# A hybrid attention and S5 layer on one core: S5 tables read from DRAM, work moved around the last gate block, the last unit's normalisations dealt out anew

## The chip, the cores and the metric

The kernel runs on one core of one Trainium2 chip. The metric is the time of one execution on the device in microseconds (us), lower is better. Its engines are TensorE (PE in the profile, with its weight loads as PEld), VectorE (DVE), ScalarE (ACT), GpSimd (POOL) and SyncE (SP), whose DMA queue the profile calls SPq.

## The reference, cut to what matters

```python
for l in range(DEPTH):
    h = _rms_norm(x, pre_norm_g[l])
    z = h @ w_in[l]
    z_q, z_kv, z_kr, g_attn, u_ssm, g_ssm = jnp.split(z, split_points, axis=-1)
    attn = _mla_attention(z_q, z_kv, z_kr, positions, q_norm_g[l], w_uq[l], kv_norm_g[l], w_ukv[l])
    attn = _rms_norm(attn, attn_out_g[l]) * jax.nn.silu(g_attn)
    ssm = _s5_bidirectional(u_ssm, s5_lam_re[l], s5_lam_im[l], s5_log_dt[l], s5_b_re[l], ...)
    ssm = jax.nn.gelu(ssm)
    ssm = ssm * jax.nn.sigmoid(ssm @ w_glu[l] + b_glu[l])
    ssm = _rms_norm(ssm, ssm_out_g[l]) * jax.nn.silu(g_ssm)
    mixed = jnp.concatenate([attn, ssm], axis=-1) @ w_out[l]
    x = x + _rms_norm(mixed, post_norm_g[l])
```

There is one layer, 2048 positions, 1024 channels, all in float32. The attention is MLA: four heads, low-rank queries (256) and keys with values (128), and a rotary key of 64 that all heads share; the softmax runs over all positions. The S5 branch has 32 groups of 16 channels, each with a complex diagonal state of 64, scanned forward and backward.

## The kernel before, in words

Each engine's instructions stand in an order written out by hand: nothing is rescheduled, and each engine takes its own list from top to bottom. A wait therefore holds whatever stands behind it on the same engine. SP issues most of the DMAs, and an issue that waits holds the issues behind it.

**Projections, 0 to 381 us.** `blocks` (line 576) yields, for each pair of tiles of 128 positions, two z blocks, two u blocks (inputs of S5, written to DRAM as `u_d`), and four gate blocks ga0, ga1, gs0, gs1 (`do_gate`, line 332). A gate block is 48 matmuls of TensorE, then a tanh (`tt`) and two scaled copies (`gst`) on ACT, then one DVE operation (line 339), then two stores `g_d<-gst` by SP (line 341). `mm3` (line 208) makes one fp32 product of three matmuls over high and low parts, so most tiles come as a pair such as `zh`, `zl`. Between the blocks, `step` (line 570) advances a generator `tables` that computes the tables of S5 on DVE. Each step adds `BUDGET` (line 50) to what the generator may spend, an amount counted in elements. It stores each table to DRAM (`tab_d`). One step of it needs matmuls, `pc` (line 540), which read scaled tables (`sc`) that DVE writes.

**The seam, 366 to 400 us.** Four quarters of the keys (`keys`, line 675, each in four stages: loads from DRAM, rope, a transposition `ptk` and its split, a transposition `ptr` and its split), the absorbed query weights (`absorbed`, line 588: `pw`, then `wab` and `wqr`) and the first queries (`qprep`, line 712) are threaded between the last gate blocks by a list of `run` calls (lines 800 to 841). The queries' pieces are: a transposition `ptq` of the loaded `zq`, its high part `zh` on ACT and its low part `zl` on DVE; two products `psr` (rope part) and four `psq` (nope part); `ta`, `tb` on DVE; two transpositions `ptr` of `qd` (line 767); and copies to `qo` on ACT and DVE. After `ph1.close()` the memory of the projections is given to the tiles of S5 and attention, so loads into it wait for what used it.

**Attention with S5, 400 to 1120 us.** Each of 256 steps `t` makes one score tile `sc` (five matmuls, lines 1111 to 1115) into one of two PSUM buffers, its maxima on DVE (`nm`, line 1116) and the Exp on ACT (line 1122), so a score tile waits for the Exp two tiles back. Eleven steps later come a transposition (line 1159) and the product with the values (lines 1179 to 1181). `s5_pre` (line 1061) adds S5's work at fixed steps. At its first call it issues the load of the tables (`s5_load`, line 864, one DMA `tab<-tab_d`), the load of the inputs (`u_load`, line 877, eight DMAs `u<-u_d`) and `u_split`, whose copy `uh<-u` on ACT (line 890) waits for all eight. The tables `v` of groups 0 to 3 are made by `v_build` (line 917) on DVE, at steps 0, 1, 3 and 4 (`V_AT`), two products and a sum each; `k_build` (line 931) multiplies them with `Bm` (`pk`, line 938) at step 6 into the lag kernels, which go to DRAM and come back as `m`, split by `m_split` (line 894) into `mh` and `ml`, which the product `py` of S5 reads.

**The end.** After the last score tile, `TAIL` (line 1542) says which engine normalises the last unit's eight tiles `e` (V is DVE, A is ACT, G is POOL), step by step; each is transposed after that (`pt`, line 1159). Then the mixer (gelu, gates, output product) runs to the end.

Of the kernel before, what the change touches and what calls it, by code (L numbers as in the profile page):

```python
# [46 lines left out]
LN2_2 = float(np.float32(math.log(2.0) - LN2_1))  # L47
GELU_C = math.sqrt(2.0 / math.pi)
GELU_A = 0.044715
BUDGET = 1800  # L50
MANUAL = {mybir.EngineType.PE, mybir.EngineType.Activation, mybir.EngineType.DVE, mybir.EngineType.Pool, mybir.EngineType.SP}


# [95 lines left out]
def tile_hymba(ctx, tc, x, pos, inv_freq, pre_g, w_in, q_g, w_uqT, w_uqr, kv_g, w_ukT, w_uv, attn_g,  # L149
# [210 lines left out]
    def s5_params():  # L360
# [63 lines left out]
        while n < T:  # L424
# [12 lines left out]
            n *= 2  # L437
            yield
        sg = Scratch(s5t, [P, NG, GH], "sc")
        for nm, w in (("qr", wr), ("qi", wi)):  # L440
            q = Scratch(s5t, [P, NG, T], "sc")()
            G.tensor_copy(q[0:64], w[0:64, :, 0:T])
            G.tensor_copy(q[64:P], w[64:P, :, 0:T][:, :, ::-1])
            store(nm, q)
        yield

        phi, ph2, ph32 = new("phi"), new("ph2"), new("ph32")
# [140 lines left out]
    def absorbed():  # L588
# [19 lines left out]
            split(wqr_h[:, k, :], wqr_l[:, k, :], raw[:, k, :], qgs[:, k:k + 1])  # L608
        yield


    xt = xp.tile([P, DM], F32, tag="xt", name="xt0")
    halves = [slice(0, 512), slice(512, DM)]
# [22 lines left out]
    for s in range(0, NT, 2):  # L636
        last = s + 2 == NT
        blk = blocks(s)
        for n in range(4 if last else 8):
            next(blk)  # L640
            if s == 0 and n == 0:
                load_w(*BLK[1])
                small_consts()
            if not last and n == 0:
                xs = [load_x(s + 2), load_x(s + 3)]
            if s == 0 and n in (1, 2):
                load_w(*BLK[1 + n])
# [23 lines left out]
    kT_h = kp.tile([P, SEQ], F32R, tag="kT_h", name="kT_h")  # L671
    kT_l = kp.tile([P, SEQ], F32R, tag="kT_l", name="kT_l")
    krS = kp.tile([P, SEQ], F32R, tag="krS", name="krS")

    def keys(q):
        t4 = slice(4 * q, 4 * q + 4)
        c = slice(q * 512, q * 512 + 512)
        zk = stg.tile([P, 4, P], F32, tag="st", name="zk")
        zr = stg.tile([P, 4, 2, HALF], F32, tag="st", name="zr")
        SP.dma_start(zk, z_d[t4, :, 256:384].rearrange("s c d -> c s d"))  # L680
        SP.dma_start(zr.rearrange("p s a b -> p s (a b)"), z_d[t4, :, 384:448].rearrange("s c d -> c s d"))
        yield
        kr2 = stg.tile([P, 4, 2, ROPE], F32, tag="st", name="kr2")
        kab = stg.tile([P, 2, 4, 2, HALF], F32, tag="tt", name="kab", bufs=2)
        V.tensor_tensor(kab[:, 0], zr, bc(ropec[:, t4, :].unsqueeze(2), [P, 4, 2, HALF]), ALU.mult)
        G.tensor_tensor(kab[:, 1], zr[:, :, ::-1, :], ropes[:, t4], ALU.mult)
        d2 = [P, 4, 2, ROPE]
        G.tensor_tensor(kr2, bc(kab[:, 0].rearrange("p s a b -> p s (a b)").unsqueeze(2), d2),
                        bc(kab[:, 1].rearrange("p s a b -> p s (a b)").unsqueeze(2), d2), ALU.add)
        A.activation(kn_h[:, t4, :], zk, AF.Copy)  # L690
        yield
        pt = psT.tile([P, 512], F32, tag="pt", name="ptk")
        for i in range(4):
            PE.transpose(pt[:, i * P:(i + 1) * P], zk[:, i, :], ident)
        split(kT_h[:, c], kT_l[:, c], pt)
        V.tensor_tensor(kn_l[:, t4, :], zk, f32(kn_h[:, t4, :]), ALU.subtract)
        yield
        pr = psZ.tile([P, 512], F32, tag="z", name="ptr")
        for i in range(4):
            PE.transpose(pr[:, i * P:(i + 1) * P], kr2[:, i].rearrange("p a b -> p (a b)"), ident)  # L700
        A.activation(krS[:, c], pr, AF.Copy)
        V.tensor_tensor(krS[64:P, c], pr[64:P, :], f32(krS[64:P, c]), ALU.subtract)
        yield


    zqs = {}
# [82 lines left out]
                    live.remove(i)  # L789
        return out  # L790

    def run(g, n):
        for _ in range(n):
            next(g)


    SP.dma_start(wuv, w_uv)
    ab = absorbed()
    ks = [keys(q) for q in range(4)]
    run(ab, 1)  # L800
    run(ks[0], 1)
    next(blk)
    run(ks[0], 1)
    run(ks[1], 1)
    next(blk)
    run(ab, 1)
    run(ks[0], 2)
    run(ks[1], 1)
    run(ks[2], 1)
    ph1g.close()  # L810
    qp = pool(ph2s, "qp", 6)
    qt_p = pool(ph2q, "qt", 1)
# [4 lines left out]
    run(ab, 1)  # L817
    q0 = qprep(0, psZ, "z")
    next(q0)
    run(ks[2], 1)  # L820
    next(blk)
    run(ks[1], 2)
    run(ks[3], 1)
    V.tensor_scalar(wuv, wuv, kvg, None, ALU.mult)
    run(ab, 1)
    run(q0, 1)
    run(ks[2], 1)
    run(ks[3], 1)
    run(q0, 1)
    next(blk)  # L830
    run(ks[2], 1)
    run(q0, 1)
    run(q0, 1)
    run(ks[3], 1)
    run(q0, 1)
    run(q0, 1)
    run(ks[3], 1)
    run(q0, 1)
    run(q0, 1)
    qo0 = []  # L840
# [76 lines left out]
    def v_build(q, i):  # L917
        f = S5[q]
        vt = s2.tile([P, 2, P], F32, tag="v", name="v", bufs=6)
        tmp = s2.tile([P, 2, P], F32, tag="tmp", name="tmp", bufs=2)  # L920
        two(G if q else V, vt, tmp, f["qr"][:, i, :], f["qi"][:, i, :], f["ct"][:, i, 0:2, :], f["ct"][:, i, 1:3, :])
        f["v"].append(vt)
        yield
        (G if q else V).tensor_tensor(vt, vt, tmp, ALU.add)

    def b_build(q):
        for p_, c in ((slice(0, 64), slice(0, GH)), (slice(64, P), slice(GH, 32))):
# [751 lines left out]
```

## Time and profile before

| what | us |
|---|---|
| median of 3 runs | 1374.33 (1373.89 to 1376.24) |
| the profiled execution's own time | 1375.26 |
| its span in the trace | 1373.5 |
| PE busy | 1340.8 |
| DVE busy | 968.0 |
| ACT busy | 818.6 |
| POOL busy | 625.6 |

The page of the profile gives each engine's busy time over the span. The waits of an engine are listed with the instruction that ended them, and the timeline gives each instruction's start and duration, with the idle time of its engine before it in brackets.

### The profile page before, as it was taken

The page shows a single profiled execution, that of the slowest core. Times are in us where ns is not written, and L with a number is a line of the kernel's source. Part 1 is how long each engine was busy: PE and PEld are TensorE (multiplying, and loading weights), DVE is VectorE, ACT ScalarE, POOL GpSimd, SP SyncE. Part 2 cuts the span into 40 slices and gives each one's busy share as a digit, 9 for nine tenths or more (in the row PEclk, how much of TensorE's full clock was granted, in tenths as well). Part 3 has the DMA queues.
Part 4 walks back from the last instruction along what each step waited for, and adds up shares of the span by engine and source line. Part 5 has one row for each costly group of instructions (what it writes and reads, how often), then busy time and mean ns, then how long its engine had stood idle before and what let it go on. Part 6 is the DMA issues. An engine that isn't in the chain of part 4 may idle for free.

```text
span 1373.5 us, 24353 instructions
## 1 busy us (share of the span) xinstructions
PE 1340.8 (98%) x9016; PEld 1217.2 (89%) x9016; DVE 968.0 (70%) x1813; ACT 818.6 (60%) x1893; POOL 625.6 (46%) x657
## 2 busy tenths in 40 slices
PE   7999999999978999999999999999999999999998
PEld 7999999999967889888888888889888888888886
DVE  6346654533288888888788789878787786877774
ACT  7422232222247878877777787778787776545542
POOL 2002311321347656675665677666552355333440
PEclk9999999999999999999999999999999999999999
DMA  8312322362541020110202102020100454455432
GB/s 304 87 46 78 86 74 62 85 143 62 129 114 26 9 52 20 41 39 5 67 9 44 32 24 44 13 63 5 33 5 9 112 149 112 126 170 179 140 107 92
DMA packets 122135, 102.93 MB, mean 75 GB/s; under 512 B 14672, under 2 KB 107104, under 8 KB 122016
## 3 DMA queue, kind: packets, MB, share of 16 engines
q1 hardware_dynamic: 110384, 89.43, 23.5%
q0 software_dynamic: 2272, 7.62, 2.2%
q10 hardware_dynamic: 9360, 4.33, 1.5%
q8 instruction: 70, 1.15, 0.4%
q14 instruction: 49, 0.40, 0.1%
HBM read 63.80 MB, written 37.54 MB: 74 GB/s over the span
## 4 chain that ended last, share of the span: by engine, by line
PE 84%; DVE 7%; issue 2%; POOL 2%; ACT 2%; DMA 1%; SPq 1%; POOLq 0%; DVEq 0%; ACTq 0%
PE pt L1159 6%; PE po L209 4%; PE po L211 4%; PE po L210 4%; PE sc L1111 4%; PE av L1181 4%; PE av L1179 4%; PE sc L1115 4%; PE av L1180 4%; PE sc L1112 4%; PE sc L1114 3%; PE sc L1113 3%; PE z_ga L211 2%; PE z_ga L210 2%; PE z_ga L209 2%
## 5 line engine op out<-in xcount | busy, mean ns | idle before, releaser
L1575 DVE TENSOR_TENSOR plo<-pt,phi 128x512 fp32r<-128x512 f32 x255 | 175.4, 688 | 57.2 <-ACT phi L1167 53.3
L1122 ACT ACTIVATE e<-sc,nm 128x512 f32<-128x512 f32 x256 | 176.1, 688 | 66.3 <-DVE nm L1116 65.4
L1116 DVE TENSOR_REDUCE nm<-sc 128x1 f32<-128x512 f32 x256 | 174.3, 681 | 50.4 <-PE sc L1115 48.7
L1167 ACT ACTIVATE phi<-pt 128x512 fp32r<-128x512 f32 x256 | 153.2, 598 | 76.0 <-PE pt L1159 75.0
L1151 ACT ACTIVATE e<-e,f 128x512 f32<-128x512 f32 x227 | 164.6, 726 | 0.4 <-DVE f L1140 0.4
L1179 PE MATMUL av<-phi,kn_h 128*128 128x256 f32 x512 | 163.5, 319 | 0.2 <-ACT avs L1184 0.2
L1159 PEld LDWEIGHTS pt<-ident,e 128*128 128x128 f32 x1024 | 126.9, 140 | 35.2 <-DVE plo L1575 1.7
L1159 PE MATMUL pt<-ident,e 128*128 128x128 f32 x1024 | 153.4, 272 | 1.7 <-DVE plo L1575 1.5
L1181 PE MATMUL av<-plo,kn_h 128*128 128x256 f32 x512 | 144.7, 283 | 0.3 <-DVE plo L1575 0.3
L1180 PE MATMUL av<-phi,kn_l 128*128 128x256 f32 x512 | 144.0, 281 | 0.0
L1111 PE MATMUL sc<-kT_h,qo 128*128 128x512 f32 x256 | 114.7, 448 | 3.3 <-ACT e L1122 1.8
L1029 POOL TENSOR_TENSOR hc<-G,t 128x512 f32<-128x512 f32 x32 | 41.9, 1310 | 136.3 <-DVE G L1573 89.8
L209 PE MATMUL po<-woh,ah 128*128 128x512 f32 (+1 forms) x264 | 101.5, 384 | 0.0
L210 PE MATMUL po<-wol,ah 128*128 128x512 f32 (+1 forms) x264 | 101.4, 384 | 0.0
L211 PE MATMUL po<-woh,al 128*128 128x512 f32 (+1 forms) x264 | 101.4, 384 | 0.0
L1112 PE MATMUL sc<-kT_l,qo 128*128 128x512 f32 x256 | 100.9, 394 | 0.0
L1114 PE MATMUL sc<-krS,qo 128*128 128x512 f32 x256 | 100.8, 394 | 0.0
L1115 PE MATMUL sc<-krS,qo 128*128 128x512 f32 x256 | 100.7, 394 | 0.0
L1113 PE MATMUL sc<-kT_h,qo 128*128 128x512 f32 x256 | 100.5, 393 | 0.0
L1179 PEld LDWEIGHTS av<-phi,kn_h 128*128 128x128 f32 x512 | 97.2, 190 | 0.5 <-ACT avs L1184 0.4
L1180 PEld LDWEIGHTS av<-phi,kn_l 128*128 128x128 f32 x512 | 97.2, 190 | 0.1
L1181 PEld LDWEIGHTS av<-plo,kn_h 128*128 128x128 f32 x512 | 96.4, 188 | 0.5 <-DVE plo L1575 0.5
(337 smaller groups left out, 4107.7 us busy)
## 6 DMA issues: line engine op xcount, KB each, us to landing
g_d<-gst SPq DMA_DIRECT2D x64, 128.0 KB, 2.0
g<-g_d SPq DMA_DIRECT2D x16, 512.0 KB, 6.0
xr<-in_x_dram SPq DMA_DIRECT2D x16, 512.0 KB, 6.6
xt<-in_x_dram SPq DMA_DIRECT2D x15, 512.0 KB, 4.0
out_dram<-res SPq DMA_DIRECT2D x15, 512.0 KB, 3.1
u_d<-ust ACTq DMA_DIRECT2D x64, 64.0 KB, 2.1
u<-u_d SPq DMA_DIRECT2D x64, 64.0 KB, 2.5
o_d<-o SPq DMA_DIRECT2D x32, 128.0 KB, 1.8
```

The lines of the kernel that those rows point to most:

```text
L209: PE.matmul(ps, ahi, bhi, start=first, stop=False)
L210: PE.matmul(ps, ahi, blo, start=False, stop=False)
L211: PE.matmul(ps, alo, bhi, start=False, stop=last)
L1111: PE.matmul(ps, qo[:, 0, w], kT_h[:, c], start=True, stop=False)
L1116: V.tensor_reduce(st["nm"][:, qt, kb:kb + 1], ps, AX.X, ALU.max, negate=True)
L1122: A.activation(e, st.pop("s"), AF.Exp, bias=st["nm"][:, qt, kb:kb + 1], accum_out=st["L"][:, qt, kb:kb + 1])
L1151: A.activation(e, e, AF.Copy, scale=f)
L1159: PE.transpose(pt[:, kk, qt, :], st["e"][qt, kt // 4][:, o:o + P], ident)
L1179: PE.matmul(o, kn_h[:, kt, :], hi[:, w], start=kt == 0, stop=False)
L1180: PE.matmul(o, kn_l[:, kt, :], hi[:, w], start=False, stop=False)
L1181: PE.matmul(o, kn_h[:, kt, :], lo[:, w], start=False, stop=kt == NT - 1)
L1575: V.tensor_tensor(lo[0], lo[1], f32(lo[2]), ALU.subtract)
```

## The change

- The tables `v` of groups 0 to 3 are computed with the other tables during the projections (six more DVE operations of 128x512 and two small copies), stored to DRAM (`v_d`, two DMAs of POOL) and read by four DMAs of SP at the first step; `v_build` issues those loads for the first quarter and computes as before, on POOL, for the others.
- `BUDGET` goes from 1800 to 1900, so the table work stands earlier between the blocks.
- `k_build(0)` runs at step 3 instead of 6, `m_split(0)` two steps sooner.
- The keys' quarters are started inside the last pair and stand one gate block sooner.
- The last gate block, gs1, moves from among the queries' pieces to behind all of them, directly before `ph1.close()`.
- `TAIL`: before, tiles 0 to 3 on DVE and ACT in the first step and 4 to 7 on POOL in the second; now all eight on DVE and ACT in turn, two in each of two steps, then one in each of four.

The body of `keys` moves unchanged and is left out here.

```diff
--- before.py
+++ after.py
@@ -47,7 +47,7 @@
 LN2_2 = float(np.float32(math.log(2.0) - LN2_1))
 GELU_C = math.sqrt(2.0 / math.pi)
 GELU_A = 0.044715
-BUDGET = 1800
+BUDGET = 1900
 MANUAL = {mybir.EngineType.PE, mybir.EngineType.Activation, mybir.EngineType.DVE, mybir.EngineType.Pool, mybir.EngineType.SP}
 
 
@@ -220,6 +220,7 @@
                   + [("bc", 16), ("bs", 16), ("rt", 1)]):
         F[nm] = 4 * n_tab, m
         n_tab += m
+    v_d = dram.tile([P, 2, 4, P], F32, tag="v_d", name="v_d")
     tab_d = dram.tile([P, NG // 4, 4 * n_tab], F32, tag="tab_d", name="tab_d")
 
 
@@ -437,11 +438,14 @@
             n *= 2
             yield
         sg = Scratch(s5t, [P, NG, GH], "sc")
+        q0 = {}
         for nm, w in (("qr", wr), ("qi", wi)):
             q = Scratch(s5t, [P, NG, T], "sc")()
             G.tensor_copy(q[0:64], w[0:64, :, 0:T])
             G.tensor_copy(q[64:P], w[64:P, :, 0:T][:, :, ::-1])
             store(nm, q)
+            q0[nm] = s5p.tile([P, 4, T], F32, tag=nm + "0", name=nm + "0")
+            e.tensor_copy(q0[nm], q[:, 0:4, :])
         yield
 
         phi, ph2, ph32 = new("phi"), new("ph2"), new("ph32")
@@ -552,9 +556,21 @@
         x1, x2 = sg(), sg()
         yield from cm(x1, x2, lbr, lbi, rawr, rawi)
         store("ct0", x1)
-        store("ct2", neg(x1, GH))
-        store("ct1", neg(x2, GH))
-        yield
+        ct = [x1, neg(x2, GH), neg(x1, GH)]
+        store("ct2", ct[2])
+        store("ct1", ct[1])
+        yield
+
+        d = [P, 4, T, GH]
+        for r in range(2):
+            p0, p1 = (Scratch(s5t, [P, 512], "sc")() for _ in range(2))
+            for p_, nm, c_ in ((p0, "qr", ct[r]), (p1, "qi", ct[r + 1])):
+                e.tensor_tensor(p_.rearrange("p (g s h) -> p g s h", g=4, s=T), bc(q0[nm].unsqueeze(3), d),
+                                bc(c_[:, 0:4, :].unsqueeze(2), d), ALU.mult)
+                yield
+            e.tensor_tensor(p0, p0, p1, ALU.add)
+            G.dma_start(v_d[:, r], p0.rearrange("p (g c) -> p g c", g=4))
+            yield
 
     def tables():
         yield from rope_tables()
@@ -607,6 +623,40 @@
             split(wab_h[:, k, :], wab_l[:, k, :], pws[k], qg[:, k:k + 1])
             split(wqr_h[:, k, :], wqr_l[:, k, :], raw[:, k, :], qgs[:, k:k + 1])
         yield
+
+    def keys(q):
...
+    def run(g, n):
+        for _ in range(n):
+            next(g)
 
 
     xt = xp.tile([P, DM], F32, tag="xt", name="xt0")
@@ -638,6 +688,10 @@
         blk = blocks(s)
         for n in range(4 if last else 8):
             next(blk)
+            if last and n == 1:
+                ab = absorbed()
+                ks = [keys(q) for q in range(4)]
+                run(ks[0], 1)
             if s == 0 and n == 0:
                 load_w(*BLK[1])
                 small_consts()
@@ -672,36 +726,6 @@
     kT_l = kp.tile([P, SEQ], F32R, tag="kT_l", name="kT_l")
     krS = kp.tile([P, SEQ], F32R, tag="krS", name="krS")
 
-    def keys(q):
...
 
     zqs = {}
 
@@ -789,24 +813,20 @@
                     live.remove(i)
         return out
 
-    def run(g, n):
-        for _ in range(n):
-            next(g)
-
 
     SP.dma_start(wuv, w_uv)
-    ab = absorbed()
-    ks = [keys(q) for q in range(4)]
     run(ab, 1)
-    run(ks[0], 1)
-    next(blk)
     run(ks[0], 1)
     run(ks[1], 1)
     next(blk)
-    run(ab, 1)
     run(ks[0], 2)
     run(ks[1], 1)
     run(ks[2], 1)
+    next(blk)
+    run(ab, 1)
+    run(ks[1], 2)
+    run(ks[2], 1)
+    run(ks[3], 1)
     ph1g.close()
     qp = pool(ph2s, "qp", 6)
     qt_p = pool(ph2q, "qt", 1)
@@ -817,31 +837,25 @@
     run(ab, 1)
     q0 = qprep(0, psZ, "z")
     next(q0)
-    run(ks[2], 1)
     next(blk)
-    run(ks[1], 2)
-    run(ks[3], 1)
+    run(ks[2], 2)
     V.tensor_scalar(wuv, wuv, kvg, None, ALU.mult)
     run(ab, 1)
-    run(q0, 1)
-    run(ks[2], 1)
-    run(ks[3], 1)
-    run(q0, 1)
-    next(blk)
-    run(ks[2], 1)
-    run(q0, 1)
     run(q0, 1)
     run(ks[3], 1)
     run(q0, 1)
     run(q0, 1)
     run(ks[3], 1)
-    run(q0, 1)
-    run(q0, 1)
+    run(q0, 2)
+    run(ks[3], 1)
+    run(q0, 3)
     qo0 = []
 
     def q0run():
         qo0.append((yield from q0))
     both(q0run())
+
+    next(blk)
     ph1.close()
     s1 = pool(s5x, "s1", 1, side="right")
     s2 = pool(s5x, "s2", 1, side="right")
@@ -917,11 +931,14 @@
     def v_build(q, i):
         f = S5[q]
         vt = s2.tile([P, 2, P], F32, tag="v", name="v", bufs=6)
+        f["v"].append(vt)
+        if q == 0:
+            SP.dma_start(vt, v_d[:, :, i, :])
+            return
         tmp = s2.tile([P, 2, P], F32, tag="tmp", name="tmp", bufs=2)
-        two(G if q else V, vt, tmp, f["qr"][:, i, :], f["qi"][:, i, :], f["ct"][:, i, 0:2, :], f["ct"][:, i, 1:3, :])
-        f["v"].append(vt)
-        yield
-        (G if q else V).tensor_tensor(vt, vt, tmp, ALU.add)
+        two(G, vt, tmp, f["qr"][:, i, :], f["qi"][:, i, :], f["ct"][:, i, 0:2, :], f["ct"][:, i, 1:3, :])
+        yield
+        G.tensor_tensor(vt, vt, tmp, ALU.add)
 
     def b_build(q):
         for p_, c in ((slice(0, 64), slice(0, GH)), (slice(64, P), slice(GH, 32))):
@@ -1055,7 +1072,7 @@
     for g_ in range(NG):
         START.append(START[-1] + (6 if g_ in (20, 21) else 7))
     PLACE = {t_: (g_, t_ - START[g_]) for g_ in range(NG) for t_ in range(START[g_], START[g_ + 1])}
-    V_AT = [0, 1, 3, 4]
+    K_AT = 3
     live, extra, mid = [], [], []
 
     def s5_pre(t):
@@ -1063,11 +1080,10 @@
             s5_load(0)
             u_load(0)
             extra.append(u_split(0, 0))
-        if t in V_AT:
-            extra.append(v_build(0, V_AT.index(t)))
+            extra.extend(v_build(0, i) for i in range(4))
         if t == 1:
             extra.append(b_build(0))
-        if t == V_AT[3] + 2:
+        if t == K_AT:
             extra.append(k_build(0))
         g, o = PLACE.get(t, (-1, 0))
         if g >= 0:
@@ -1078,7 +1094,7 @@
                     s5_load(q + 1)
             if i == 1 and o == 3:
                 extra.append(u_split(q, 1))
-            if i == 1 and o == (4 if q == 0 else 0):
+            if i == 1 and o == (2 if q == 0 else 0):
                 extra.append(m_split(q))
             if q > 0 and i == 0 and o == 1:
                 extra.append(k_build(q))
@@ -1539,7 +1555,7 @@
     QOFF = {0, 1, 2, 4, 5, 6}
     s5_pre(-1)
     p3 = None
-    TAIL = [[(0, "V"), (1, "A"), (2, "V"), (3, "A")], [(k, "G") for k in range(4, 8)]]
+    TAIL = [[(0, "V"), (1, "A")], [(2, "V"), (3, "A")], [(4, "V")], [(5, "A")], [(6, "V")], [(7, "A")]]
     for t in range(8 * NU + LAG + AVLAG + 2):
         n, i = divmod(t, 8)
```

**TensorE at the seam.** These are the rows of PE from the transposition of the first queries to the first score tile; `z_gs` is the gate block gs1 (48 rows, the first shown), `psr` and `psq` the first row of the first product of each. Before:

```order
L721 MATMUL ptq<-ident,zq 128x128 x4
L694 MATMUL ptk<-ident,zk 128x128 x4
L209 MATMUL z_gs<-hh,wh_gs 128x256
...
L700 MATMUL ptr<-ident,kr_4388 128x128 x4
L209 MATMUL psr<-wqr_h,zh 128x256
...
L209 MATMUL psq<-zh,wab_h 128x256
...
L767 MATMUL ptr_4649<-ident,qd 128x128 x4
L767 MATMUL ptr_4662<-ident,qd 128x128 x4
L1111 MATMUL sc<-kT_h,qo_0_4609 128x512
```

The same stretch of the change:

```order
L745 MATMUL ptq<-ident,zq 128x128 x4
L209 MATMUL psr<-wqr_h,zh 128x256
...
L646 MATMUL ptk<-ident,zk 128x128 x4
...
L209 MATMUL psq<-zh,wab_h 128x256
...
L791 MATMUL ptr_4609<-ident,qd 128x128 x4
L791 MATMUL ptr_4622<-ident,qd 128x128 x4
L209 MATMUL z_gs<-hh,wh_gs 128x256
...
L1127 MATMUL sc<-kT_h,qo_0_4569 128x512
```

The gate block stood between the transposition `ptq` and the products that read its split; now it stands between the last transposition of the queries and the first score tile, and the first `psr` follows `ptq` at once.

**SP and ACT ahead of the first Exp.** On SP the gate block's two stores stand ahead of the loads of S5; on ACT its three instructions and the copy `uh` stand ahead of the first Exp (`e,L<-sc,nm`). Before, SP and then ACT:

```order
L680 DMA zk<-z_d 128x4x128
L681 DMA zr<-z_d 128x4x64
L710 DMA zq<-z_d 128x2x256
L341 DMA g_d<-gst 128x2x128 x2
L867 DMA tab_4724<-tab_d 128x964
L881 DMA u_0_4726<-u_d 16x8x128 x8
L710 DMA zq<-z_d 128x2x256
```

```order
L335 ACTIVATE tt<-z_gs 128x512
L338 ACTIVATE gst<-z_gs,outg 128x256 x2
L701 ACTIVATE krS<-ptr 128x512
...
L739 ACTIVATE qo_0_4609<-psq,kvgs 128x256
...
L770 ACTIVATE qo_3_4639<-ptr_4662 128x128
L890 ACTIVATE uh<-u_0_4726 128x2x256
L1122 ACTIVATE e,L<-sc,nm 128x512
L727 ACTIVATE zh<-ptq 128x512
```

Of the change, SP and then ACT:

```order
L734 DMA zq<-z_d 128x2x256
L342 DMA g_d<-gst 128x2x128 x2
L881 DMA tab_4741<-tab_d 128x964
L895 DMA u_0_4743<-u_d 16x8x128 x8
L936 DMA v<-v_d 128x2x128 x4
L734 DMA zq<-z_d 128x2x256
```

```order
L763 ACTIVATE qo_0_4569<-psq,kvgs 128x256
...
L794 ACTIVATE qo_3_4599<-ptr_4622 128x128
L336 ACTIVATE tt<-z_gs 128x512
L339 ACTIVATE gst<-z_gs,outg 128x256 x2
L904 ACTIVATE uh<-u_0_4743 128x2x256
L1138 ACTIVATE e,L<-sc,nm 128x512
L751 ACTIVATE zh<-ptq 128x512
```

The order on SP is the same but for the four loads of `v`; on ACT the gate block's three instructions now stand right before `uh`, and all the queries' copies ahead of them.

**VectorE ahead of the table matmuls.** The matmuls `pc` read the result of the DVE rows `sc<-sc` 128x512 of line 69. Before, on DVE:

```order
L275 TENSOR_SCALAR xt_3504<-xt_3504,rr 128x1024
L69 TENSOR_SCALAR sc<-sc 128x512
L339 SCALAR_TENSOR_TENSOR gst<-tt,gst 128x512 x2
L69 TENSOR_SCALAR sc<-sc 128x512
L339 SCALAR_TENSOR_TENSOR gst<-tt,gst 128x512 x2
```

Of the change:

```order
L276 TENSOR_SCALAR xt_3519<-xt_3519,rr 128x1024
L195 TENSOR_SCALAR rv<-ss 128x1
L276 TENSOR_SCALAR xt_3521<-xt_3521,rr 128x1024
L69 TENSOR_SCALAR sc<-sc 128x512
L340 SCALAR_TENSOR_TENSOR gst<-tt,gst 128x512 x3
L69 SCALAR_TENSOR_TENSOR sc<-ident,dsk,pc 128x128 x4
```

On PE `pc` moves from between gs0 and gs1 of the last pair but one to between its ga0 and ga1, two gate blocks sooner; on DVE the scaled table that it reads now stands behind both scalings of the next pair's inputs.

## Rows read from the trace of the kernel before

**Rows 1.** The page: busy time of TensorE, share of the span, instructions.

```profile
PE 1340.8 (98%) x9016; PEld 1217.2 (89%) x9016; DVE 968.0 (70%) x1813; ACT 818.6 (60%) x1893; POOL 625.6 (46%) x657
```

**Rows 2.** Windows: length, each engine's busy us (instructions), granted clock, DMA share, GB/s.

```profile
100.00:381.00 281.00, 281.00 (x2136) 275.42 (x2135) 129.06 (x340) 81.47 (x196) 71.56 (x92) 1.00 0.36 90
```

**Rows 3.** Waits of PE, 381 to 460 us: total us, times, longest.

```profile
PE psq L209 <- DVE tb L756: 1.9, 2, 1.1
PE ptq L721 <- DMA zq<-z_d: 1.7, 1, 1.7
PE pk L938 <- DVE v L924: 1.7, 1, 1.7
PE py L211 <- POOL ml L898: 1.7, 1, 1.7
PE sc L1111 <- DVE qo L773: 1.3, 1, 1.3
PE psr L209 <- DVE zl L729: 1.0, 1, 1.0
PE sc L1111 <- ACT e L1122: 0.9, 2, 0.5
PE psr L211 <- DVE zl L729: 0.4, 1, 0.4
```

**Rows 4.** Timeline of PE: start, us, instruction, [idle before <-releaser].

```profile
383.83 0.37 PE L209 MATMUL z_gs<-hh,wh_gs 128*128 128x256 f32 x1
...
399.77 0.47 PE L1111 MATMUL sc<-kT_h,qo 128*128 128x512 f32 x1 [1.34 <-DVE qo L773]
...
402.76 0.50 PE L1111 MATMUL sc<-kT_h,qo 128*128 128x512 f32 x1
```

**Rows 5.** Timeline of ACT, gate block gs1 to the first Exp.

```profile
389.86 0.60 ACT L335 ACTIVATE tt<-z_gs 128x512 f32<-128x512 f32 x1 [1.19 <-PE z_gs L211]
...
400.75 0.63 ACT L890 ACTIVATE uh<-u 128x512 fp32r<-128x512 f32 x1 [1.36 <-DMA u<-u_d]
401.93 0.69 ACT L1122 ACTIVATE e<-sc,nm 128x512 f32<-128x512 f32 x1 [0.55 <-DVE nm L1116]
402.52 0.19 ACT L1122 ACTIVATION_READ_ACCUMULATOR e<-sc,nm 128x1 f32 x1
```

**Rows 6.** Timeline of SP's queue, the same stretch (issues).

```profile
392.28 0.87 SPq L341 DMA_DIRECT2D g_d<-gst  x2
...
393.81 4.53 SPq L881 DMA_DIRECT2D u<-u_d  x8
```

**Rows 7.** Timeline of DVE behind the split of the first queries' weights.

```profile
388.33 0.68 DVE L203 TENSOR_TENSOR kT_l<-ptk,kT_h 128x512 fp32r<-128x512 f32 x1
388.93 0.98 DVE L696 TENSOR_TENSOR kn_l<-zk,kn_h 128x512 fp32r<-128x512 f32 x1
389.84 0.41 DVE L685 TENSOR_TENSOR kab<-zr,ropec 128x256 f32<-128x256 f32 x1
390.17 0.68 DVE L729 TENSOR_TENSOR zl<-ptq,zh 128x512 fp32r<-128x512 f32 x1
```

**Rows 8.** Timeline of DVE around 313 us, inputs and tables.

```profile
313.08 0.75 DVE L275 TENSOR_SCALAR xt<-xt,rr 128x1024 f32<-128x1024 f32 x1 [0.67 <-POOL rr L196]
313.75 0.77 DVE L69 TENSOR_SCALAR sc<-sc 128x512 f32<-128x512 f32 x1
```

**Rows 9.** The last unit: waits of PE (1100 to 1145 us), then DVE and POOL.

```profile
PE pt L1159 <- DVE plo L1575: 1.5, 1, 1.5
...
1119.07 0.48 DVE L1147 TENSOR_SCALAR e<-e,f 128x512 f32<-128x512 f32 x1
...
1123.33 2.13 DVE L1147 TENSOR_SCALAR e<-e,f 128x512 f32<-128x512 f32 x2
...
1122.95 4.85 POOL L1149 TENSOR_TENSOR e<-e,f 128x512 f32<-128x512 f32 x4 [1.97 <-DVE f L1140]
```

**Rows 10.** Timeline of PE near the span's start; windows near its end.

```profile
8.68 0.74 PE L209 MATMUL z_z<-wh_z,hh 128*128 128x448 f32 x1 [0.30 <-ACT hh L202]
...
12.20 0.36 PE L209 MATMUL z_z<-wh_z,hh 128*128 128x448 f32 x1
...
13.20 0.37 PE L211 MATMUL z_z<-wh_z,hl 128*128 128x448 f32 x1
...
1366.00:1368.00 2.00, 0.80 (x7) 0.59 (x5) 0.95 (x3) 0.51 (x2) 0.00 (x0) 1.00 0.00 0
1370.50:1371.00 0.50, 0.00 (x0) 0.00 (x0) 0.00 (x0) 0.00 (x0) 0.00 (x0) 0.58 1.00 373
```

More of the change, by code (lines that the diff above doesn't have):

```diff
@@ L609, in absorbed @@
         yield
+    def keys(q):
+        t4 = slice(4 * q, 4 * q + 4)
+        c = slice(q * 512, q * 512 + 512)
+        zk = stg.tile([P, 4, P], F32, tag="st", name="zk")
+        zr = stg.tile([P, 4, 2, HALF], F32, tag="st", name="zr")
+        SP.dma_start(zk, z_d[t4, :, 256:384].rearrange("s c d -> c s d"))
+        SP.dma_start(zr.rearrange("p s a b -> p s (a b)"), z_d[t4, :, 384:448].rearrange("s c d -> c s d"))
+        yield
+        kr2 = stg.tile([P, 4, 2, ROPE], F32, tag="st", name="kr2")
+        kab = stg.tile([P, 2, 4, 2, HALF], F32, tag="tt", name="kab", bufs=2)
+        V.tensor_tensor(kab[:, 0], zr, bc(ropec[:, t4, :].unsqueeze(2), [P, 4, 2, HALF]), ALU.mult)
+        G.tensor_tensor(kab[:, 1], zr[:, :, ::-1, :], ropes[:, t4], ALU.mult)
+        d2 = [P, 4, 2, ROPE]
+        G.tensor_tensor(kr2, bc(kab[:, 0].rearrange("p s a b -> p s (a b)").unsqueeze(2), d2),
+                        bc(kab[:, 1].rearrange("p s a b -> p s (a b)").unsqueeze(2), d2), ALU.add)
+        A.activation(kn_h[:, t4, :], zk, AF.Copy)
+        yield
+        pt = psT.tile([P, 512], F32, tag="pt", name="ptk")
+        for i in range(4):
+            PE.transpose(pt[:, i * P:(i + 1) * P], zk[:, i, :], ident)
+        split(kT_h[:, c], kT_l[:, c], pt)
+        V.tensor_tensor(kn_l[:, t4, :], zk, f32(kn_h[:, t4, :]), ALU.subtract)
+        yield
+        pr = psZ.tile([P, 512], F32, tag="z", name="ptr")
+        for i in range(4):
+            PE.transpose(pr[:, i * P:(i + 1) * P], kr2[:, i].rearrange("p a b -> p (a b)"), ident)
+        A.activation(krS[:, c], pr, AF.Copy)
+        V.tensor_tensor(krS[64:P, c], pr[64:P, :], f32(krS[64:P, c]), ALU.subtract)
+        yield
+    def run(g, n):
+        for _ in range(n):
+            next(g)
     xt = xp.tile([P, DM], F32, tag="xt", name="xt0")
@@ L673, in tile_hymba @@
     krS = kp.tile([P, SEQ], F32R, tag="krS", name="krS")
-    def keys(q):
[L676 to L681, printed above, removed]
-        yield
[L683 to L690, printed above, removed]
-        yield
[L692 to L703, printed above, removed]
     zqs = {}
```

## The prediction

> **What bounds the kernel now.** I read the page's first part first: TensorE is busy 1340.8 of a span of 1373.5 us [rows 1]. All other engines have spare time on average, so the time is TensorE's work, which this change leaves as it is, and its waits, 32.7 us in all. I therefore asked of each edit only which wait of TensorE it makes, shortens or moves. The windows show where a new wait can't hide: from 100 to 381 us TensorE is busy throughout [rows 2], so a wait put there is added whole. The list of its waits from 381 to 460 us, the stretch that most of the edits touch, comes to 1.9 + 1.7 + 1.7 + 1.7 + 1.3 + 1.0 + 0.9 + 0.4 = 10.6 us [rows 3]: all that the change could win there. Then I read the timelines of the engines on which those waits end, and held the orders of before and after against them.
>
> The sum is made against the profiled execution, 1375.26 us; it lies 0.93 above the median of 1374.33, and I apply the difference to the median. About 0.2% (2.7 us) is what a measurement of this kernel can tell from no change.
>
> **Part 1, the table matmuls two gate blocks sooner (budget).** In the trace the first gate block of that pair ends near 313.3 on TensorE, and `pc` now follows at once. It reads a scaled table that DVE makes behind the scaling of the next inputs: those two rows stand at 313.08 (0.75) and 313.75 (0.77) [rows 8]. So the table is there near 314.3 to 314.5, and TensorE waits some 0.9 us (bounds 0 if the tables run further ahead, 1.2 if they don't), with no idle time later in that stretch to absorb it [rows 2]. **+0.9.** The six other table operations and two copies run on a DVE that is busy 129 of 281 us there [rows 2]; if that cover failed, eight rows of 0.7 us would come on the path, but what TensorE needs of DVE there is made a block ahead. Zero.
>
> **Part 2, the queries lose their cover.** Before, gs1 (383.83 to 389.66, which is 5.8 us) ran on TensorE while ACT and DVE made `zh` and `zl` out of `ptq`; the wait left was 0.4 [rows 3, 4]. Now the first `psr` follows `ptq` at once, and its third matmul needs `zl`. DVE starts `zl` at 390.17 behind a chain without gaps [rows 7]; the change takes `kT_l` and `kn_l` (starts 0.60 and 0.91 apart) out from ahead of it, so `zl` ends near 390.85 - 1.5 = 389.35. TensorE, ready at about 384.1, does two matmuls and waits till then: about 4.9 us. Behind it I expect 0.4 on `tb` and 1.7 in two parts on the rotation of `qd`, instead of 1.1 on `tb` before (its second wait, 0.8, is a later one). The 1.3 on `qo` is covered by gs1, which now stands there. So 4.9 + 0.4 + 1.7 against 0.4 + 1.1 + 1.3: **+4.2**, of which I take **+3.8**, as some of the keys' work has gone a block earlier; bounds 2.8 and 4.5.
>
> **Part 3, the first Exp behind the gate block's stores.** This decides. On ACT the copy `uh` stands before the first Exp; it waits for eight loads of `u`, which SP issues behind gs1's two stores and the table load. Before, from the end of gs1 on TensorE (389.66) over the stores (392.28) and the loads (393.81, 4.53 for eight issues) to the end of `uh` (401.38) are 11.7 us [rows 4 to 6]. They were hidden, because the queries' products ran meanwhile: the Exp at 401.93 waited for its maxima, not for `uh` [rows 5]. Now gs1 comes last, so the same 11.7 us begin where the first score tile begins. The Exp adds 0.69 + 0.19 [rows 5], so the third score tile, which needs the first tile's buffer, can start 12.6 us after gs1. TensorE has two score tiles and a transposition to do meanwhile, 402.76 - 399.77 = 3.0 us [rows 4]. What is left is a wait of **+9.6** us. Bounds: if the eight loads were issued without gaps and landed as in a quiet queue, some 2 us less; if the first load also had to wait for the stores to land, 1.0 to 1.5 us more.
>
> **Part 4, a long idle of TensorE and its clock.** Before, no wait in the stretch is longer than 1.7 us [rows 3]. Near the start of the span, after 6.4 us without work, nine matmuls of 448 columns take 12.20 - 8.68 = 3.52 us, and the five behind them 1.00 us, 0.20 each [rows 10]: nine at that pace are 1.8, so the cold start cost 1.7 us there. At the end TensorE's last matmul lies before 1368 and the granted clock is at 1.00, and in 1370.5 to 1371 it is 0.58, on the way from 2.4 to 1.2 GHz [rows 10]. A wait of 9.6 us is longer than that idle, so I add the same **+1.7** (bounds 0 and 2.7, with the eight transpositions ahead of those nine at half pace too). The Trainium skill, TensorE: Matmul & The Clock Gate, HAM oscillation, says that an idle that is too long throttles the engine, so that the work behind it starts cold; the trace agrees at its two ends, and no row of before shows it in the middle. By the rule the sum keeps its 1.7 us, and without it the forecast would be 1382.5.
>
> **Part 5, what comes back.** Behind the third score tile TensorE waited 1.0 (`zl`), 1.7 (`pk` for `v`), 1.7 (`py` for `ml`), 0.9 (Exp) and 0.8 (`tb`), 6.1 us in all [rows 3]. After a wait of 9 us DVE and POOL have caught up, and `v` comes by DMA, the lag kernels sooner: I take **-4.8** (all but the Exp's and part of `tb`'s), bounds -6.1 and -3. The four loads of `v` follow `u` on SP at some 0.4 us an issue, and hold only the next `zq`, which is needed many steps later.
>
> **Part 6, the end.** Two normalisations on DVE took 2.13 us beside four on POOL (4.85 us), against 0.48 for one alone, and TensorE waited 1.5 us for the `plo` behind them [rows 9]. Without POOL's four, DVE does two more at 0.48 and ACT two more, spread over steps. I take **-1.3** (bounds -2.2 and 0: the waits may return one by one).
>
> **Sum.** 0.9 + 3.8 + 9.6 + 1.7 - 4.8 - 1.3 = +9.9: about 1385.2 for the profiled execution, **1384.2** on the median. Steps 460 to 1100 keep their order; I put nothing there.
>
> **Rivals.**
> 1. *Faster: the loads run beside gs1, and ACT is not held.* If `u` is in place when the first score tile is (about 404), parts 3 and 4 fall away: then 0.9 + 3.8 - 4.8 - 1.3 = -1.4, and with the returns at their full bounds (-6.1, -2.2) and part 2 at 2.8, it is -4.6: **1369.7**. For it: the loads read `u_d`, which was written long before. Against it: SP takes its list in order, and the stores of gs1, which wait for DVE's `gst`, stand ahead of `u` in both orders. It decides at the time at which SP issues the first `u`: before 396 or after 405. Chance 0.07.
> 2. *No change.* The same with the returns as I took them, about -1.4: **1373**, or a shorter hold that the returns just pay for. Chance 0.05.
> 3. *The loads take longer.* `u` lands beside `tab` and `v` on one set of DMA engines, the first `u` waits for the stores to land, and the returns are small because the Exp chain on ACT, not DVE, sets the pace behind the wait: 0.9 + 4.5 + 11.1 + 2.7 - 3 - 0.8 = +15.4: **1389.7**. Chance 0.13.
> 4. *The change doesn't do what it says for `pk`:* `v` by DMA lands behind `u`, so `pk` would wait for the DMA as it did for DVE; +1.7 on the forecast, **1385.9**. Within the forecast's case.
>
> **How the numbers follow.** The forecast's case has 0.75, rival 3 0.13; both are slower, and in either the gain of rival 1 is excluded by the order on two engines. Slower 0.88, same 0.05, faster 0.07. The lower end takes part 3 two us lower, the clock at 0 and the returns somewhat larger: 1384.2 - 2 - 1.7 - 2 = **1378.5**; the upper end takes in most of rival 3: **1388**. Below lie rivals 1 and 2, 0.12, and some 0.08 lies above.
>
> **What would show it.** In the trace of the changed kernel: a wait of TensorE of 8 to 11 us before the third score tile, ended by ACT, and `uh` right before the first Exp with a wait for `u`; a wait of 4 to 5 us at the first `psr` on `zl`; about 0.9 us at `pc`; no waits on `v` and little on `ml`; matmuls at half pace behind the long wait. The forecast is wrong if `u` is issued before gs1 has ended, or if the third score tile starts within 2 us of the second's end.

## The result and the profile after

| | us |
|---|---|
| before, median of 4 runs | 1375.28 (1373.89 to 1377.08) |
| the change, median of 4 runs | 1386.67 (1385.79 to 1388.96) |
| ratio, 95% interval | 1.0084, 1.0071 to 1.0096 |
| span of the profiled execution | 1373.5 before, 1384.0 after |

The change is slower, by 11.4 us between the medians and by 10.5 us between the two profiled spans. The forecast was +9.9.

The page's busy times after, beside [rows 1]:

```profile
PE 1345.5 (97%) x9016; PEld 1220.4 (88%) x9016; DVE 962.7 (70%) x1811; ACT 818.9 (59%) x1895; POOL 618.7 (45%) x655
```

TensorE does the same 9016 instructions but is busy for 4.7 us more: some of them ran slower. The other 5.8 us of the 10.5 are waits. TensorE's waits from 381 to 460 us, as [rows 3] had them (total, times, longest):

```profile
PE sc L1127 <- ACT e L1138: 9.8, 2, 9.4
PE psr L209 <- ACT zh L751: 2.7, 1, 2.7
PE psr L211 <- DVE zl L753: 1.4, 1, 1.4
PE ptq L745 <- DMA zq<-z_d: 0.6, 1, 0.6
PE psr L210 <- DVE wqr_l L206: 0.6, 1, 0.6
PE ptr L791 <- POOL qd L783: 0.6, 1, 0.6
PE psq L209 <- DVE tb L780: 0.5, 1, 0.5
PE psq L209 <- DVE qo L765: 0.4, 1, 0.4
```

One wait of 9.4 us and three at the first `psr` (2.7 + 0.6 + 1.4 = 4.7) are new; those on `v`, `ml` and `qo` before the first score tile are gone. The timeline of ACT and of SP's queue show how the long one comes about, beside [rows 5] and [rows 6]:

```profile
404.41 0.60 ACT L336 ACTIVATE tt<-z_gs 128x512 f32<-128x512 f32 x1 [4.98 <-PE z_gs L211]
...
415.15 0.63 ACT L904 ACTIVATE uh<-u 128x512 fp32r<-128x512 f32 x1 [9.41 <-DMA u<-u_d]
415.69 0.67 ACT L1138 ACTIVATE e<-sc,nm 128x512 f32<-128x512 f32 x1
```

```profile
406.49 0.87 SPq L342 DMA_DIRECT2D g_d<-gst  x2
407.59 0.33 SPq L881 DMA_DIRECT2D tab<-tab_d  x1
409.01 3.64 SPq L895 DMA_DIRECT2D u<-u_d  x8
412.81 2.54 SPq L936 DMA_DIRECT2D v<-v_d  x4
```

The gate block ends at 404.2, its stores are issued at 406.49, the loads of `u` from 409.01, and `uh` can start at 415.15; ACT has idled for 9.41 us, with the first Exp right behind `uh`. SP's own list of waits from 392 to 412 us names what stood between the load of the tables and the first load of `u`, the landing of the gate block's stores:

```profile
SPq L895 <- DMA g_d<-gst: 1.0, 1, 1.0
```

Before, SP issued the first `u` right behind the tables. On TensorE the following rows are the end of the second score tile, then the third and the fourth, beside [rows 4]:

```profile
406.74 0.39 PE L1131 MATMUL sc<-krS,qo 128*128 128x512 f32 x1
416.50 0.79 PE L1127 MATMUL sc<-kT_h,qo 128*128 128x512 f32 x1 [9.38 <-ACT e L1138]
417.09 0.63 PE L1128 MATMUL sc<-kT_l,qo 128*128 128x512 f32 x1
...
421.18 0.50 PE L1127 MATMUL sc<-kT_h,qo 128*128 128x512 f32 x1
421.52 0.40 PE L1128 MATMUL sc<-kT_l,qo 128*128 128x512 f32 x1
```

Behind the wait the matmuls of a tile stand 0.43 us apart, at 421.18 again 0.23. The windows name the reason (columns as in [rows 2]; the clock is the third number from the end):

```profile
384.00:386.00 2.00, 0.00 (x0) 0.00 (x0) 1.97 (x4) 2.00 (x6) 0.00 (x0) 1.00 0.49 132
386.00:388.00 2.00, 0.75 (x2) 0.47 (x2) 1.97 (x4) 1.08 (x3) 0.00 (x0) 0.73 0.45 130
388.00:390.00 2.00, 0.59 (x2) 0.37 (x2) 1.57 (x4) 0.00 (x0) 0.71 (x1) 0.50 0.00 0
390.00:392.00 2.00, 2.00 (x11) 2.00 (x11) 0.00 (x0) 0.26 (x1) 0.57 (x1) 0.50 0.00 0
394.00:396.00 2.00, 2.00 (x19) 2.00 (x19) 1.22 (x3) 1.43 (x3) 1.29 (x1) 1.00 0.00 0
...
410.00:412.00 2.00, 0.00 (x0) 0.00 (x0) 0.00 (x0) 0.00 (x0) 0.00 (x0) 0.71 0.80 254
412.00:414.00 2.00, 0.00 (x0) 0.00 (x0) 0.00 (x0) 0.00 (x0) 0.00 (x0) 0.50 0.88 133
...
418.00:420.00 2.00, 2.00 (x9) 1.79 (x7) 0.69 (x1) 0.24 (x1) 0.98 (x2) 0.50 0.64 235
421.00:422.00 1.00, 1.00 (x12) 0.69 (x5) 0.00 (x0) 0.28 (x1) 0.00 (x0) 0.97 0.00 0
```

The granted clock falls to 0.50 (1.2 GHz) twice: behind the first of the three waits at the first `psr`, and in the long wait. The matmuls' spacing has it back at 393.8 and 421.2 us, with TensorE at work without a pause since 389.6 and 416.5.

**How to add it up.** Each kernel has the same 256 score tiles in the same order, so the start of a tile's first matmul minus that of the same tile before says how far TensorE is behind at that place. In us, for before absolute, for the others the difference:

| tile | before | change | gs1_back | uh_late | uh_k_late | v_dve | fill40 | best |
|---|---|---|---|---|---|---|---|---|
| (z at 249 us) | 249.03 | -0.40 | -0.24 | +0.18 | -0.12 | +0.37 | -0.20 | +0.33 |
| 1st | 399.77 | +4.44 | -1.72 | +5.22 | +5.02 | -1.21 | +4.96 | -2.36 |
| 3rd | 402.76 | +13.74 | -0.06 | +5.95 | +5.75 | +0.60 | +14.06 | -1.90 |
| 4th | 405.97 | +15.21 | -0.56 | +13.32 | +4.58 | -0.58 | +13.57 | -2.38 |
| 21st | 450.09 | +10.63 | -5.05 | +10.17 | +3.87 | -0.56 | +8.99 | -6.35 |
| 129th | 761.57 | +10.59 | -5.09 | +10.24 | +3.88 | -0.59 | +8.93 | -6.34 |
| last | 1118.28 | +10.51 | -2.09 | +13.28 | +3.90 | +0.29 | +9.07 | -5.52 |

The first row is a matmul of the projections, `z_z<-wh_z,hl`, that stands ahead of all that the edits move on TensorE. Its differences were there within 30 us of the start, and they say how far two executions differ for no reason of the edits: up to 0.4 us. In the change, then, 4.4 + 0.4 = 4.8 us are lost up to the first tile.

The column of the change is the whole story: +4.4 at the first tile, +9.3 in the long wait, +1.5 and more at half pace, -4.6 back up to the 21st, and nothing later. (The 3 us between the 129th and the last tile in gs1_back and uh_late, and the 0.9 in v_dve, come from a meeting of two engines that the last section tells of. The 0.8 in best was not followed up.)

### The profile page after: what moved, and what is told of

It is laid out like the page before. It is cut to its first block, busy times and chain, and to the rows that moved or that the text cites. A ratio compares the mean times of both kernels' runs of the same rounds, so it can differ in the third digit from the quotient of the medians.

```text
span 1384.0 us, 24356 instructions
## 1 busy us (share of the span) xinstructions
PE 1345.5 (97%) x9016; PEld 1220.4 (88%) x9016; DVE 962.7 (70%) x1811; ACT 818.9 (59%) x1895; POOL 618.7 (45%) x655
## 4 chain that ended last, share of the span: by engine, by line
PE 82%; DVE 6%; ACT 3%; DMA 2%; POOL 2%; issue 2%; SPq 1%; ACTq 0%; DVEq 0%; POOLq 0%
PE pt L1175 6%; PE sc L1127 4%; PE po L209 4%; PE po L211 4%; PE po L210 4%; PE av L1197 4%; PE sc L1131 3%; PE av L1195 3%; PE sc L1128 3%; PE sc L1130 3%; PE sc L1129 3%; PE av L1196 3%; PE z_gs L211 2%; PE z_gs L209 2%; PE z_gs L210 2%
## 5 line engine op out<-in xcount | busy, mean ns | idle before, releaser
L1127 PE MATMUL sc<-kT_h,qo 128*128 128x512 f32 x256 | 115.2, 450 | 10.8 <-ACT e L1138 10.5
```

What stands on the lines that cost most here:

```text
L1127: PE.matmul(ps, qo[:, 0, w], kT_h[:, c], start=True, stop=False)
```

## The experiments

**gs1_back** moves the last gate block back between the queries' transposition and their products, and leaves all else of the change.

```diff
     run(ks[3], 1)
     run(q0, 1)
+    next(blk)
     run(q0, 1)
...
     both(q0run())
-
-    next(blk)
     ph1.close()
```

> The change, but with the last gate block back between the queries' transposition and their products. My theory (the gate block's place makes the long wait, through its stores, the loads of u and the copy uh, and takes the cover from the queries' splits): the wait of 9.4 us before the third score tile and the 4.7 us before the first psr go, TensorE never idles long enough to lose its clock (4.7 us of extra busy time in the changed kernel), and what the other edits win stays: about 1370 us, 4 to 6 us below the kernel before. Rival (the waits that vanished behind the long wait were only absorbed by it): about 1375 us, the kernel before.

Measured: 1373.02 us against 1375.49 for before (ratio 0.998, 0.997 to 0.999), 2.5 us less and not the 4 to 6 expected. At the 21st and the 129th tile it is some 5 us ahead of before, the amount expected; 3.0 us of it are lost near 836 us in the profiled run, for a reason of its own. Its waits of 381 to 460 us:

```profile
PE sc L1126 <- ACT e L1137: 2.1, 2, 1.6
PE psq L209 <- DVE tb L780: 0.7, 2, 0.5
PE ptr L791 <- POOL qd L783: 0.6, 1, 0.6
PE ptr L791 <- DVE tb L780: 0.6, 1, 0.6
PE ptq L745 <- DMA zq<-z_d: 0.5, 1, 0.5
PE psq L209 <- DVE qo L765: 0.5, 1, 0.5
```

The waits on `zh`, `zl`, `v` and `ml` are absent. So the gate block's place alone turns a gain of 5 us at the 21st tile into a loss of 10.6, and the rival falls: what vanished behind the long wait is won without it too.

**v_dve** takes gs1_back and makes `v` on DVE again, with the lag kernels at step 6 and their split as before.

```diff
-        if q == 0:
-            SP.dma_start(vt, v_d[:, :, i, :])
-            return
...
-            extra.extend(v_build(0, i) for i in range(4))
+        if t in (0, 1, 3, 4):
+            extra.append(v_build(0, (0, 1, 3, 4).index(t)))
...
-    K_AT = 3
+    K_AT = 6
```

> gs1_back, but with the tables v of groups 0 to 3 made on DVE at steps 0, 1, 3 and 4, the lag kernels at step 6 and their split as before (the tables are still stored and not read). Theory (the gain behind the first tiles is v from DRAM and the lag kernels sooner): the waits of TensorE on v (1.7), zl (1.0) and ml (1.7) are back, and the score tiles from the 20th on stand 3 to 4.5 us later than in gs1_back, at -2 to -0.5 us against the kernel before. Rival (the gain comes from the keys' work a block sooner): they stay within 1 us of gs1_back.

Measured: 1375.8 us in one run, and -0.56 at the 21st tile against -5.05. Two of the three waits that I expected are back, that on `zl` is not:

```profile
PE py L211 <- POOL ml L911: 1.7, 1, 1.7
PE pk L951 <- DVE v L937: 1.7, 1, 1.7
```

From the first tile to the 21st gs1_back gains 3.3 us and v_dve loses 0.65. So the tables from DRAM with the lag kernels sooner are worth 4.0 us; the other 0.5 of the 4.5 between the two kernels is there at the first tile already, and comes from the executions' starts (+0.37 and -0.24 at 249 us). What both gain ahead of the first tile, 1.5 to 1.6 us against their own starts, is put down to the keys' work a block sooner, less the wait at `pc`; no run has either of these alone.

**uh_late** puts the copy `uh` on ACT behind the first six Exps.

```diff
-            extra.append(u_split(0, 0))
             extra.extend(v_build(0, i) for i in range(4))
...
+        if t == 6:
+            extra.append(u_split(0, 0))
```

> The change, but with the copy uh on ACT seven steps later (step 6), so that it stands behind the first six Exps. If ACT's order alone makes the wait, the third score tile follows the second at once and the time falls by 9 to 12 us, to about 1375 us. My theory: the wait moves to TensorE's pk, which at step 3 needs v, the last loads of the same queue (landed near 418 us): 7 to 9 us of wait remain, the clock still falls, and the time is 1383 to 1386 us.

Measured: 1386.69 us (ratio 1.0081, 1.0064 to 1.0098), no gain. The wait before the third tile is 0.81 us, so ACT's order did make the long wait; but the fourth stands at +13.32, because `pk` now meets the same queue:

```profile
416.28 3.08 PE L955 MATMUL pk<-v,Bm 128*32 128x128 f32 x16 [5.37 <-DMA v<-v_d]
419.29 0.80 PE L1128 MATMUL sc<-kT_h,qo 128*128 128x512 f32 x1
```

The wait on `v` is 5.4 us, less than the 7 to 9 I expected, but `pk` itself takes 3.08 us instead of 0.66 in gs1_back: its 16 short matmuls start in four groups, at 416.28, 416.94, 417.62 and 418.30, each within 0.15 us of the landing of its table, and the clock is at 0.50 there.

**uh_k_late** also moves the lag kernels from step 3 to step 7 and their split two steps later.

```diff
-    K_AT = 3
+    K_AT = 7
...
-            if i == 1 and o == (2 if q == 0 else 0):
+            if i == 1 and o == (4 if q == 0 else 0):
```

> The change, with uh at step 6 and the lag kernels at step 7 instead of 3 (their split two steps later, as before the change). My theory: now neither ACT nor pk meets the late loads; the long wait and its half pace go, 1 to 3 us of waits on v and ml come back: 1375 to 1378 us. If the late loads hold TensorE by a third way (tables, Bm, ul), over 1380 us.

Measured: 1381.21 us (ratio 1.0045, 1.003 to 1.006), a miss by 3 us. The number is that of my second case, but no wait on a late load is behind it. The long wait and its half pace are gone, as expected: +5.0 at the first tile, +3.9 at the 21st. What I had left out is the loss at the queries, which this edit doesn't touch. The wait on `ml` that the change had removed came back whole, and `pk` waited 2.0 us again, now for `wTl`, another table made by DVE, and not for `v`:

```profile
PE pk L955 <- DVE wTl L203: 2.0, 1, 2.0
PE sc L1128 <- ACT e L1139: 1.7, 3, 0.8
PE py L211 <- POOL ml L912: 1.7, 1, 1.7
```

**fill and fill40** put matmuls whose results nobody reads into the long wait, before the third score tile; they differ in the count.

```diff
+            if t == 2:
+                fill = psP.tile([P, 2, 2, P], F32, tag="p", name="fill").rearrange("p a b c -> p (a b c)")
+                for _ in range(32):
+                    PE.matmul(fill, kT_h[:, 0:P], kT_h[:, 0:512], start=True, stop=True)
             scores(qo[b][h], sts[n], i)
```

> The change, with 32 matmuls of 512 columns into an unused PSUM tile put on TensorE ahead of the third score tile (their results are not used); at 0.23 us each they take 7.4 of the 9.4 us of the long wait. Theory (the half pace behind the wait is the clock, which falls because TensorE idles): the granted clock stays at 1.00 there, five score matmuls take 0.23 us each instead of 0.43, and the time falls by 2 to 2.5 us, to about 1384 us. Rival (the slower pace comes from the loads' traffic or the weights): no fall, or a rise.

Measured with 32: 1386.6 us (ratio 1.0082, 1.0067 to 1.0097), no fall. The test had not kept the clock up:

```profile
414.00:416.00 2.00, 0.85 (x4) 0.38 (x2) 0.00 (x0) 0.44 (x1) 0.00 (x0) 1.00 0.55 140
416.00:418.00 2.00, 1.09 (x5) 0.86 (x5) 0.62 (x1) 2.00 (x6) 1.67 (x3) 1.00 0.77 221
418.00:420.00 2.00, 2.00 (x17) 1.65 (x19) 0.77 (x2) 0.80 (x3) 1.33 (x3) 0.58 0.90 275
```

The filling ended at 414.9, TensorE waited 2.1 us, worked on from 416.9, and fell to 0.50 at 418.3 while it worked. Hence the second try:

> The fill again with 40 matmuls instead of 32 (9.2 us), so that TensorE doesn't idle before the third score tile; with 32 the clock fell after all, some 2 us behind the filling, over the 2.1 us of wait that were left. If the clock is what made tiles three and four slow, the granted clock is 1.00 from 404 to 425 us and the fourth score tile starts 2 to 2.5 us behind the third instead of 4.7. Whether that reaches the later tiles is open: if it does, the 20th tile stands at +8.5 us against the kernel before instead of +10.6; if the Exps on ACT set the pace there, it stays at +10.5.

Measured with 40: 1383.5 us in one run. The clock stays at 1.00, and the fourth tile starts 2.7 us behind the third instead of 4.7:

```profile
416.00:418.00 2.00, 1.90 (x9) 1.12 (x7) 0.69 (x1) 1.93 (x6) 1.76 (x3) 1.00 0.74 197
418.00:420.00 2.00, 2.00 (x26) 1.59 (x25) 0.69 (x1) 0.97 (x3) 1.25 (x3) 1.00 0.91 283
```

It reaches the later tiles: from the first to the 21st tile the loss is 8.99 - 4.96 = 4.0 us instead of 10.63 - 4.44 = 6.2. So the clock behind the long wait costs 2.0 to 2.2 us; 0.2 of the difference is there at the third tile already (9.1 us behind the first instead of 9.3), and each kernel has one traced execution. The loads and the weights are the same in both kernels, so the rival falls.

**tail_only** is the kernel before with the new `TAIL` alone.

```diff
-    TAIL = [[(0, "V"), (1, "A"), (2, "V"), (3, "A")], [(k, "G") for k in range(4, 8)]]
+    TAIL = [[(0, "V"), (1, "A")], [(2, "V"), (3, "A")], [(4, "V")], [(5, "A")], [(6, "V")], [(7, "A")]]
```

> The kernel before with the new division of the last eight normalisations alone. The timelines of before and of the change, laid on each other, say that the wait of 1.5 us on plo shrinks to 0.2 and three waits behind it give most of that back: TensorE's last product of the attention is 0.2 to 0.5 us earlier against the last score tile than in before. My prediction had put 1.3 us there.

Measured: 1375.1 us in one run. TensorE's timeline in the last unit:

```profile
1124.69 0.66 PE L1159 MATMUL pt<-ident,e 128*128 128x128 f32 x4 [0.21 <-DVE plo L1575]
...
1128.50 0.39 PE L1179 MATMUL av<-phi,kn_h 128*128 128x256 f32 x1 [0.47 <-ACT avs L1184]
...
1132.35 0.38 PE L1181 MATMUL av<-plo,kn_h 128*128 128x256 f32 x1 [0.62 <-DVE plo L1575]
...
1144.15 0.70 PE L1188 MATMUL po<-avs,wuv 128*128 128x256 f32 x2 [0.47 <-ACT avs L1184]
```

In before these four stand at 1126.11, 1129.34, 1132.86 and 1144.65, and its last score tile is 0.13 later; so the new order is 1.3 us ahead at the first, 0.7, 0.4, and 0.4 at the last. The wait on `plo` [rows 9] did go from 1.5 to 0.2; the normalisations that left POOL now stand on ACT and DVE between the copies that the next products need, and 0.9 us are given back. The mixer takes the rest: from the last score tile to the end of the span tail_only is 0.1 us faster than before, and the change, gs1_back, v_dve and best lie between 0.2 faster and 0.2 slower.

**best** follows from gs1_back: `v` is loaded ahead of `u`, `uh` comes at step 4, and a budget of 1840 puts `pc` back between gs0 and gs1.

```diff
-BUDGET = 1900
+BUDGET = 1840
...
-            u_load(0)
-            extra.append(u_split(0, 0))
-            extra.extend(v_build(0, i) for i in range(4))
+            for i in range(4):
+                next(v_build(0, i), None)
+            u_load(0)
...
+        if t == 4:
+            extra.append(u_split(0, 0))
```

> gs1_back with three more edits: the loads of v ahead of those of u, uh at step 4 instead of ahead of the first Exp, and a budget of 1840, which puts the table matmuls pc back between gs0 and gs1. The theory that in gs1_back uh still holds the third score tile (1.6 us) and pc still waits for its table (1.0 us): both waits go, and the shift of the score tiles against the kernel before grows from -5.0 to -7 or -7.6 us; about 1368 us. Rival: pk, at step 3, now meets the loads of v and takes 1 to 1.5 us of it back: shift -6.

Measured: 1369.42 us against 1374.81 for before (ratio 0.996, 0.9946 to 0.9974), faster than both kernels. At the 21st tile it is 6.35 us ahead, 6.7 against its own start. `pc` and `pk` wait no more; the wait of the third tile went from 1.6 to 0.4 us, not to nothing, so the gain lies between the two cases.

## Why the prediction was right

The sign, the size and the place were as forecast, and the mechanism of part 3, on which it rested, is shown by gs1_back and uh_late. That the sum came so near is partly luck: errors cancel inside parts 2 and 3, and part 6 was wrong. Against its steps:

- **Part 1, `pc`: +0.6** where 0.9 was forecast, and 0.6 to 1.0 in the seven kernels with this budget. DVE's second row took 0.42 us, not 0.77, in the new place.
- **Part 2, the queries: +4.2.** The first tile stands at +4.44; with the 0.40 by which the execution was ahead from its start, and without 0.62 at `pc`, this is 4.2, and so it is in uh_late, uh_k_late, fill and fill40. This is the sum as first written (4.2), from which 0.4 was then taken off for the keys' work, without a row. But it came about by other terms. The waits at the first `psr` came to 4.73 us (4.9), but the forecast had all of it on `zl`, and 2.7 were ended by `zh`: on ACT it stood behind four splits of the absorbed weights. Then three errors cancel: the waits on `tb` and `qd` were 0.6, not 2.1; the wait on `zq` ahead of it shrank from 1.7 to 0.6, since its load is issued sooner; and the half pace from 387 to 393.8 us, which I had not thought of here, cost some 1.9 us (4.19 us from the third `psr` matmul to the second of `psq`, against 2.29 for the same stretch before and in gs1_back).
- **Part 3, the first Exp: +9.3** (9.6). Here too errors cancel: SP's wait for the stores to land, which the forecast had as a bound only, made the first `u` 1.0 us later against the stores, while the stores came 0.3 us sooner behind gs1 and the stretch from the first `u` to the end of `uh` was 0.8 us shorter.
- **Part 4, the clock: +2.0 to 2.2** (1.7) behind the long wait, by fill40. The Trainium skill, TensorE: Matmul & The Clock Gate, HAM oscillation, says that a long idle throttles the engine and that what follows starts cold; the trace now agrees in the middle of the kernel, with 0.50 from 412 us on.
- **Part 5, the returns: -5.1 to -5.3** (13.74 + 2.2 - 10.63 = 5.3) where 4.8 was taken and 6.1 was the bound.
- **Part 6, the end: 0.0** (1.3): the step that failed. At the last product of the attention 0.3 to 0.4 us were left of the 1.3, at the end of the span nothing (10.5 at the last score tile, 10.5 between the spans). I counted the wait that would go and not what comes behind it: eight normalisations on two engines that TensorE waits for anyway.

From the start to the 21st tile this is -0.4 + 0.6 + 4.2 + 9.3 + 2.2 - 5.3 = +10.6; the spans differ by 10.5. The rivals: the loads could not run beside gs1 (rival 1), as the first `u` was issued at 409.01, behind its end at 404.2; and `pk` did not wait in the change (rival 4) because the longer wait before it covered its loads. In uh_late, where that cover is gone, rival 4's wait is there, with 5.4 us.

## What to carry to other kernels

When a block of work is moved to cover a wait, follow everything that it issues on every queue, to the last consumer: here a gate block that hid 1.3 us put its two stores, and behind them the load of the tables and the eight of `u`, on the path to the first Exp. A load that is late should have its consumer late too, on all engines: moving one consumer only hands the wait to the next. And a wait of TensorE is priced with the clock behind it, here some 2 us at each of two places.

## What was not expected of the hardware

- **The clock falls at waits much shorter than the long one.** At the first `psr` the granted clock went from 1.00 to 0.50 at 386.9 us, behind one wait of 2.7 us; the next two came at the lower clock. In fill it fell at 418.3 us, behind a wait of 2.1 us and 1.4 us of work. The length of one wait does not tell it: near 851 us in fill it fell behind a wait of 1.9 us, and in uh_k_late it stayed at 1.00 behind one of 2.0 us. Before the change the longest wait here was 1.7 us, and the clock stayed.
- **A chance meeting of DVE and POOL costs up to 3.0 us.** In four of the ten profiled executions (gs1_back, uh_late, fill, v_dve) the 155th score tile waits 1.7 to 2.3 us for an Exp, instead of 0.7 to 0.9. In the first three the clock falls behind it, and TensorE is 2.6 to 3.0 us later; in v_dve, with the shortest of these waits, the clock stays at 1.00 and the loss is 0.9 us. In gs1_back DVE, POOL and then TensorE read:

```profile
830.95 1.20 DVE L1151 TENSOR_TENSOR L<-L,f 128x8 f32<-128x8 f32 x1
...
830.82 1.31 POOL L905 TENSOR_TENSOR ul<-u,uh 128x512 fp32r<-128x512 f32 x1 [2.43 <-ACT uh L903]
...
835.93 0.80 PE L1126 MATMUL sc<-kT_h,qo 128*128 128x512 f32 x1 [2.26 <-ACT e L1137]
```

  An operation of 8 columns, which takes 0.15 to 0.16 us in the six other executions, ends with POOL's operation, and the maxima behind it are late. The Trainium skill, SBUF — State Buffer, "SBUF: two separate sides", says that DVE with two inputs in SBUF and POOL lock one pair of ports for a whole instruction; the two rows, which end at 832.15 and 832.13, agree. The order of the two starts goes with it: in the four executions DVE's operation starts 0.03 to 0.17 us behind POOL's, in the six others ahead of it or within 0.01 us. What sets that order was not tried. The times of gs1_back (1370.1 to 1375.2 in ten runs) may spread for this reason, so the tiles' starts were used beside the medians.
